# Other durations in the planner that orders a two-layer transformer on one core, and one buffer moved from weight sums to raw weights

## The chip, the cores and the metric

The kernel runs on one core of one Trainium2 chip. The metric is the device time of one execution in microseconds (us). The core has five engines that run side by side, each with an in-order queue of its own: PE (matmuls; the profile lists its weight loads apart, as PEld), DVE (element-wise work), ACT (element-wise functions, casts, copies out of PSUM), POOL and SP. Here SP issues every transfer between the chip's memory and the on-chip SBUF. Matmul results land in PSUM, eight banks of 128x512 numbers, and are read out by DVE or ACT. Engines wait for each other through semaphores.

## The reference

Two layers on 1024 tokens of width 1024, all in float32. Layer 0 mixes with sliding-window attention, layer 1 with a chunked linear recurrence (HGRN2); each is followed by a squared-ReLU MLP of width 4096.

```python
for layer in range(DEPTH):                       # DEPTH = 2
    h = rmsnorm(x, mix_norm[layer])
    if layer % 2 == 0:
        y = sliding_window_attention(h, positions, attn_w_qkv[0], attn_b_qkv[0], attn_sinks[0], attn_w_o[0])
    else:
        y = hgrn2_recurrence(h, lbs[layer], hgrn_w_in[0], hgrn_g_norm[0], hgrn_w_o[0])
    x = x + y
    h = rmsnorm(x, mlp_norm[layer])
    x = x + jnp.square(jax.nn.relu(h @ mlp_w_up[layer])) @ mlp_w_down[layer]
return rmsnorm(x, final_norm)
```

## The kernel before

**Arithmetic.** Activations lie as tiles of 128 features by 512 tokens (two halves of the sequence). A float32 product is made of three matmuls in the faster float32r format: each operand is split into a high part and the rest (`wh`, `wl` for a weight, two `a` or `t` tiles for an activation), and `mm3` adds high x high, high x rest and rest x high into one PSUM bank. `weight_split` makes `wh` by a cast (on ACT or on DVE, whichever the planner picks) and `wl` by a subtraction on DVE. The MLPs and the recurrence's input projection use Strassen's scheme (seven products for eight), in the up projections once more on some leaves; so weights are first added to each other (`strassen_weights`: sums s1 to s4 and the inner ones), and products are added up again by DVE.

**Stages in order of time.** Attention's projections and blocks (`qkv`, `attend`, `o_proj`), the first MLP (`pair_first`, `pair`, then `down`), the recurrence (`gates` and `recurrence`, one head after the other, interleaved), its output projection (`hgrn_out`), the second MLP, the final norm. Neighbouring stages overlap where their data allow.

**Buffers.** `BUFS` gives the number of SBUF tiles of each kind: 60 `a`, 18 `t`, 7 `m` (weight sums; also the softmax's scores and other short-lived tiles), 5 `wr` (raw weights as they come from memory), 5 `wh`, 5 `wl`; and 4 + 4 PSUM banks (`p`, `q`).

**What sets the order.** Nothing is issued while the code above runs: every operation is recorded with its engine (or two possible engines), a duration and what it reads and writes. `Schedule.order` then plays a list schedule: again and again it takes the engine that is free first, and of the operations that are ready there by its clock the one of lowest rank (program order; weights come 100 places earlier). A transfer occupies SP for its cost, and its data count as there `tail` later:

```python
            if op.form and op.form != form:
                form, t = op.form, t + DRAIN[op.form]
            free_at[e] = t + cost
            end = t + cost + op.tail
...
            for o in op.after:
                met(o, end + max(LATENCY[e][w] for w in o.ways))
...
                    heapq.heappush(slots[key], (b.freed + 200.0, b.slot))
```

The last line gives a buffer back when its last user has ended by that clock: a tile that is being stored keeps its slot until the planned landing of the store, and the next tile of that kind takes the slot that came free first. So the durations decide three things: the order in each engine's queue, the engine of each cast, and which slot a new tile gets, thus whose end it waits for on the chip. `DRAIN` is added in the plan where PE changes between matmuls that fill all 128 columns ("whole") and those that use half of them ("columns": attention's values and the recurrence's chunks). The order is then fixed in the program; on the chip each queue runs in that order, whatever the real durations are.

Of the kernel before, what the change touches and what calls it, by code (L numbers as in the profile page):

```python
# [37 lines left out]
MAGIC = 12582912.0  # L38
TWO_PI = (6.28125, 2029.0 / 2**20, 2 * np.pi - 6.28125 - 2029.0 / 2**20)
PI_DOWN = float(np.float32(3.1415925))  # L40
BUFS = {"a": 60, "t": 18, "m": 7, "sm": 8, "wr": 5, "wh": 5, "wl": 5, "p": 4, "q": 4}
CH = 64
LEVELS = 6
HOMES = "aaaaaaaaaaaa"
# [87 lines left out]
    "Pool": {"SP": 200.0, "PE": 190.0, "ACT": 75.0, "DVE": 74.0, "Pool": 102.0},  # L132
}
WEIGH = 1.0
DRAIN = {"whole": 120.0, "columns": 120.0}
LEAD = 100
WARM = 8
EVACUATE = 100
# [3 lines left out]
class Schedule:  # L142
# [42 lines left out]
    def order(self):  # L185
# [35 lines left out]
        while True:  # L221
# [36 lines left out]
# [3 lines that stand above are left out]
# [21 lines left out]
class Net:  # L282
# [38 lines left out]
    def a(self, dt=F32, shape=(P, TH)):  # L321
        return self.tile("a", BUFS["a"], shape, dt)

    def t(self, dt=F32, shape=(P, TH), tag="t"):
        return self.tile(tag, BUFS[tag], shape, dt)

    def psum(self, tag="p"):
        return self.tile(tag, BUFS[tag], (P, TH), F32, self.pp)

# [14 lines left out]
        return d  # L344

    def dma(self, out, in_, nbytes):
        self.op("SP", self.nc.sync.dma_start, [out], [in_], max(650.0, nbytes / 320.0), out, in_, tail=2000.0)

    def memset(self, out, value, e="DVE", late=()):
        self.op(e, self.engine(e).memset, [out], list(late), 300, out, value)  # L350
# [37 lines left out]

    def mm(self, out, lhsT, rhs, start, stop, n=TH, rate=1.0, form="whole", late=(), **kw):

        cost = n * rate / (2.25 if rate == 1.0 else 2.4) + 4
        self.op("PE", self.nc.tensor.matmul, [out], [lhsT, rhs, *late], cost, out, lhsT, rhs, start=start, stop=stop, form=form, **kw)

    def mm3(self, out, w, x, start, stop, n=TH, **kw):
# [12 lines left out]
    def raw(self, src):  # L407
        r = self.tile("wr", BUFS["wr"], (P, TH), F32)
        self.dma(r, src, 4 * P * TH)
        return r  # L410

    def weight_split(self, z):
        hi, lo = (self.tile(tag, BUFS[tag], (P, TH), F32R) for tag in ("wh", "wl"))
        self.copy(hi, z, TH, ("ACT", "DVE"), False)
        self.tt("any", lo, z, hi.bitcast(F32), ALU.subtract)
        return hi, lo
# [56 lines left out]
    def lay_out(self):  # L473
# [3 lines left out]
        for tag in ("a", "t", "wr", "wh", "wl"):  # L477
            for k in range(BUFS[tag]):
                self.pool.tile([P, TH], F32, tag=f"{tag}_{k}", name=f"{tag}_first{k}", bufs=1)
# [1175 lines left out]
```

## Time and profile before

| | |
|---|---|
| time, median of 3 runs | 2098.83 us (2096.93 to 2103.28) |
| the profiled execution's own time, and its span from first to last instruction | 2103.77 us, 2102.0 us |
| PE busy | 2068.4 us, 98% of the span, 12220 matmuls |
| DVE busy | 1898.4 us, 90% |
| ACT busy | 1120.0 us, 53% |
| transfers | 407.43 MB, 194 GB/s over the span |

The stages in the span, by the tiles that the trace shows: attention to about 350 us, first MLP to about 950 us, recurrence to about 1400 us, its output projection to about 1500 us, second MLP and final norm to 2102 us. All instructions carry the line of one helper (L336), so the profile is read by tile names and by time. A row of a view by time gives start, duration, engine, instruction, out<-in and, in square brackets, how long the engine stood idle before it and what ended that.

### The profile page before, as it was taken

The page shows a single profiled execution, that of the slowest core. Times are in us where ns is not written, and L with a number is a line of the kernel's source. Part 1 is how long each engine was busy: PE and PEld are TensorE (multiplying, and loading weights), DVE is VectorE, ACT ScalarE, POOL GpSimd, SP SyncE. Part 2 cuts the span into 40 slices and gives each one's busy share as a digit, 9 for nine tenths or more (in the row PEclk, how much of TensorE's full clock was granted, in tenths as well). Part 3 has the DMA queues.
Part 4 walks back from the last instruction along what each step waited for, and adds up shares of the span by engine and source line. Part 5 has one row for each costly group of instructions (what it writes and reads, how often), then busy time and mean ns, then how long its engine had stood idle before and what let it go on. Part 6 is the DMA issues. An engine that isn't in the chain of part 4 may idle for free.

```text
span 2102.0 us, 35648 instructions
## 1 busy us (share of the span) xinstructions
PE 2068.4 (98%) x12220; PEld 1738.6 (83%) x12220; DVE 1898.4 (90%) x3922; ACT 1120.0 (53%) x2284; POOL 61.0 (3%) x121
## 2 busy tenths in 40 slices
PE   9999999999999999999999999999999999999998
PEld 7778777888888887888888888888788888888887
DVE  8889899999999989999889888888999999998995
ACT  5567777656565323556444444443755656432453
POOL 4030000000000000000000000000000000000000
PEclk9999999999999999999999999999999999999999
DMA  6212277867778967732322232576787777896742
GB/s 214 79 51 81 86 239 245 297 224 248 231 240 289 313 220 245 236 136 76 101 98 99 96 101 97 202 234 221 270 267 229 244 228 250 284 321 211 238 133 80
DMA packets 225845, 407.43 MB, mean 194 GB/s; under 512 B 25344, under 2 KB 30464, under 8 KB 225664
## 3 DMA queue, kind: packets, MB, share of 16 engines
q1 hardware_dynamic: 225664, 405.16, 58.5%
q8 instruction: 96, 1.57, 0.3%
q14 instruction: 85, 0.70, 0.1%
HBM read 321.17 MB, written 83.89 MB: 193 GB/s over the span
## 4 chain that ended last, share of the span: by engine, by line
PE 38%; DVE 11%; DMA 4%; issue 3%; ACT 1%; POOL 0%; SPq 0%; POOLq 0%; DVEq 0%; ACTq 0%
PE p L336 22%; PE q L336 16%; DVE t L336 4%; DVE a L336 3%; DMA wr<-in_down 2%; DVE wl L336 2%; DVE m L336 2%; ACT t L336 1%; DMA t<-d 1%; DMA wr<-in_up 1%; DMA d<-t 0%; DVE wh L336 0%; DMA wr<-in_win 0%; DMA a<-d 0%; ACT wh L336 0%
## 5 line engine op out<-in xcount | busy, mean ns | idle before, releaser
L336 PE MATMUL p<-a,wh 128*128 128x512 f32 (+1 forms) x2880 | 809.9, 365 | 3.2 <-DVE a L336 2.4
L336 PE MATMUL q<-a,wh 128*128 128x512 f32 x2112 | 654.6, 391 | 7.4 <-ACT t L336 6.1
L336 PEld LDWEIGHTS p<-a,wh 128*128 128x128 f32 x2880 | 514.6, 189 | 89.1 <-DVE a L336 4.0
L336 PE MATMUL p<-a,wl 128*128 128x512 f32 (+1 forms) x1440 | 521.0, 362 | 0.4 <-DVE wl L336 0.4
L336 PEld LDWEIGHTS q<-a,wh 128*128 128x128 f32 x2112 | 389.1, 188 | 85.3 <-ACT t L336 8.4
L336 PE MATMUL q<-a,wl 128*128 128x512 f32 x1056 | 411.1, 390 | 1.7 <-DVE wl L336 1.7
L336 PEld LDWEIGHTS p<-a,wl 128*128 128x128 f32 x1440 | 271.6, 189 | 40.9 <-DVE wl L336 1.3
L336 DVE TENSOR_TENSOR wl<-wr,wh 128x512 fp32r<-128x512 f32 x352 | 240.8, 685 | 6.7 <-ACT wh L336 1.3
L336 DVE TENSOR_TENSOR wl<-m,wh 128x512 fp32r<-128x512 f32 x338 | 230.1, 686 | 10.6 <-ACT wh L336 1.4
L336 PEld LDWEIGHTS q<-a,wl 128*128 128x128 f32 x1056 | 198.3, 188 | 45.6 <-DVE wl L336 3.7
L336 ACT ACTIVATE t<-t 128x512 f32<-128x512 f32 x268 | 168.8, 632 | 122.3 <-DVE t L336 114.9
L336 ACT CAST wh<-wr 128x512 fp32r<-128x512 f32 x249 | 154.0, 619 | 142.8 <-PE p L336 94.7
L336 DVE TENSOR_TENSOR t<-t,t 128x512 f32<-128x512 f32 (+3 forms) x337 | 197.4, 599 | 17.0 <-DMA t<-d 9.9
L336 ACT CAST a<-t 128x512 fp32r<-128x512 f32 (+1 forms) x216 | 130.1, 611 | 148.5 <-PE q L336 78.7
L336 DVE TENSOR_TENSOR a<-t,a 128x512 fp32r<-128x512 f32 (+2 forms) x314 | 205.9, 677 | 2.2 <-ACT a L336 1.7
L336 ACT CAST wh<-m 128x512 fp32r<-128x512 f32 x231 | 143.1, 620 | 113.8 <-PE p L336 47.4
L336 ACT COPY t<-q 128x512 f32<-128x512 f32 (+2 forms) x201 | 112.2, 559 | 104.1 <-PE q L336 87.3
L336 DVE TENSOR_TENSOR m<-wr,wr 128x512 f32<-128x512 f32 (+1 forms) x188 | 120.9, 645 | 17.6 <-DMA wr<-in_down 13.0
L336 PE MATMUL p<-wh,a 128*128 128x512 f32 x384 | 124.9, 396 | 0.7 <-ACT a L336 0.7
L336 DVE TENSOR_TENSOR t<-t,p 128x256 f32<-128x256 f32 x294 | 118.0, 414 | 0.3
L336 PEld LDWEIGHTS q<-t,t 128*64 128x64 f32 (+1 forms) x2160 | 95.4, 144 | 13.6 <-issue 7.6
L336 PE MATMUL q<-t,t 128*64 128x32 f32 (+2 forms) x2160 | 105.3, 229 | 0.0
(129 smaller groups left out, 2392.7 us busy)
## 6 DMA issues: line engine op xcount, KB each, us to landing
t<-d SPq DMA_DIRECT2D x548, 256.0 KB, 4.1
d<-t SPq DMA_DIRECT2D x244, 256.0 KB, 2.7
wr<-in_down SPq DMA_DIRECT2D x224, 256.0 KB, 4.2
wr<-in_up SPq DMA_DIRECT2D x178, 256.0 KB, 3.9
wr<-in_win SPq DMA_DIRECT2D x68, 256.0 KB, 2.9
a<-d SPq DMA_DIRECT2D x60, 256.0 KB, 4.7
wr<-in_wqkv SPq DMA_DIRECT2D x48, 256.0 KB, 2.9
d<-a SPq DMA_DIRECT2D x48, 256.0 KB, 3.9
```

Of the source, the lines that this page charges most:

```text
L336: fn(*[place(a) for a in args], **{k: place(v) for k, v in kw.items()})
```

## The change

Numbers of the plan change, and two of the buffer counts; no operation is added or taken away.

```diff
-BUFS = {"a": 60, "t": 18, "m": 7, "sm": 8, "wr": 5, "wh": 5, "wl": 5, "p": 4, "q": 4}
+BUFS = {"a": 60, "t": 18, "m": 6, "sm": 8, "wr": 6, "wh": 5, "wl": 5, "p": 4, "q": 4}
...
-DRAIN = {"whole": 120.0, "columns": 120.0}
+DRAIN = {"whole": 200.0, "columns": 200.0}
+FULL = {512: 227.3, 256: 119.8}
...
     def dma(self, out, in_, nbytes):
-        self.op("SP", ..., max(650.0, nbytes / 320.0), out, in_, tail=2000.0)
+        self.op("SP", ..., max(450.0, nbytes / 320.0), out, in_, tail=2750.0)
...
     def mm(self, out, lhsT, rhs, start, stop, n=TH, rate=1.0, form="whole", late=(), **kw):
-        cost = n * rate / (2.25 if rate == 1.0 else 2.4) + 4
+        cost = FULL.get(n, n / 2.25 + 4) if rate == 1.0 else n * rate / 2.4 + 4
```

In the plan, a float32r matmul over 512 columns now lasts 227.3 ns where it lasted 231.6, over 256 columns 119.8 where it was 117.8; a transfer's data come 2750 ns after its issue's end where it was 2000; an issue lasts at least 450 ns where it was 650 (a transfer of 256 KB stays at 262144 / 320 = 819 ns, so only small ones change); a change of form costs 200 ns where it was 120. A sixth raw weight tile is loaded ahead in `first_loads`, and one weight sum fewer can be alive.

What this does to the queues, at two places. The digits before the underscore number a tile; they are the same in both kernels there.

The start of the second MLP, ACT's queue, before. `q4300` is a PSUM bank with a finished product; the copy into `t4302` empties it so that PE can go on.

```order
L336 ACTIVATE t4230_17987<-q4092_17552 128x512
L336 COPY a4240_17996<-t4236_17886 128x512
L336 COPY wh4322_18002<-wr4315_17897 128x512
L336 COPY t4260_18018<-t4248_17903 128x512
L336 COPY t4268_18026<-t4249_17993 128x512
L336 COPY wh4324_18032<-m4311_17946 128x512
L336 COPY t4303_18043<-q4301_17998 128x512
L336 COPY t4302_18057<-q4300_17930 128x512
L336 COPY t4264_18065<-t4248_17903 128x512
```

The same place after the change:

```order
L337 ACTIVATE t4230_17982<-q4092_17541 128x512
L337 COPY a4240_17991<-t4236_17886 128x512
L337 COPY wh4322_17997<-wr4315_17892 128x512
L337 COPY t4260_18014<-t4248_17932 128x512
L337 COPY t4302_18022<-q4300_17927 128x512
L337 COPY wh4324_18028<-m4311_17963 128x512
L337 COPY t4268_18039<-t4249_18011 128x512
L337 COPY t4264_18056<-t4248_17932 128x512
L337 COPY t4304_18071<-q4300_17927 128x512
L337 COPY t4303_18083<-q4301_17993 128x512
```

The copy out of `q4300` moved three rows forward. The slot of `t4302` changed too: before, it was that of `t4230`, and the copy had to wait until the store of `t4230` to memory had landed; now it is a slot whose last user is a DVE operation.

PE's queue at the same place, before (the matmuls from `wh4296` on write `q4300` again, so they wait for that copy):

```order
L336 MATMUL q4340_18034<-a3939_16732,wh4320_17981 128x512
L336 MATMUL q4340_18034<-a3940_16766,wh4320_17981 128x512
L336 MATMUL p4343_18041<-a3955_16857,wh4322_18002 128x256
L336 MATMUL p4343_18041<-a3956_16867,wh4322_18002 128x256
L336 MATMUL p4344_18046<-a3963_16968,wh4322_18002 128x256
L336 MATMUL p4344_18046<-a3964_16978,wh4322_18002 128x256
L336 MATMUL q4341_18052<-a4098_17188,wh4324_18032 128x512
L336 MATMUL q4341_18052<-a4099_17203,wh4324_18032 128x512
L336 MATMUL q4300_17930<-a4128_17330,wh4296_17906 128x512
L336 MATMUL q4300_17930<-a4129_17340,wh4296_17906 128x512
```

And after:

```order
L337 MATMUL q4340_18030<-a3939_16744,wh4320_17973 128x512
L337 MATMUL q4340_18030<-a3940_16766,wh4320_17973 128x512
L337 MATMUL q4300_17927<-a4128_17351,wh4296_17899 128x512
L337 MATMUL q4300_17927<-a4129_17376,wh4296_17899 128x512
L337 MATMUL q4300_17927<-a4128_17351,wl4297_17911 128x512
L337 MATMUL q4300_17927<-a4130_17399,wh4296_17899 128x512
L337 MATMUL q4300_17927<-a4131_17439,wh4296_17899 128x512
L337 MATMUL q4300_17927<-a4130_17399,wl4297_17911 128x512
```

The six matmuls into `p4343`, `p4344` and `q4341` moved behind the twelve that write `q4300`.

The end of the recurrence's output projection, DVE's queue, before. `m4211` is a weight sum of the second MLP, for which ACT and PE wait; the `a` tiles are splits of activations, `t4160` a sum of squares.

```order
L336 TENSOR_TENSOR t4156_17494<-t4156_17494,t4109_17313 128x512
L336 TENSOR_TENSOR t4160_17522<-t4160_17522,t4161_17529 128x512
L336 TENSOR_TENSOR m4210_17699<-wr4208_17514,wr4209_17536 128x512
L336 TENSOR_TENSOR a4154_17706<-t4152_17474,a4153_17691 128x512
L336 TENSOR_TENSOR t4160_17522<-t4160_17522,t4162_17550 128x512
L336 TENSOR_TENSOR a4158_17718<-t4156_17494,a4157_17708 128x512
L336 TENSOR_TENSOR t4160_17522<-t4160_17522,t4163_17600 128x512
L336 TENSOR_TENSOR m4211_17730<-m4210_17699,wr4206_17485 128x512
```

And after:

```order
L337 TENSOR_TENSOR t4156_17528<-t4156_17528,t4109_17308 128x512
L337 TENSOR_TENSOR a4137_17673<-t4096_17111,a4136_17657 128x512
L337 TENSOR_TENSOR a4150_17678<-t4148_17487,a4149_17664 128x512
L337 TENSOR_TENSOR wl4197_17684<-wr4183_17406,wh4196_17676 128x512
L337 TENSOR_TENSOR t4160_17586<-t4160_17586,t4161_17623 128x512
L337 TENSOR_TENSOR a4154_17696<-t4152_17507,a4153_17686 128x512
L337 TENSOR_TENSOR a4158_17703<-t4156_17528,a4157_17693 128x512
L337 TENSOR_TENSOR t4160_17586<-t4160_17586,t4162_17594 128x512
L337 TENSOR_TENSOR m4210_17715<-wr4208_17479,wr4209_17494 128x512
L337 TENSOR_TENSOR t4160_17586<-t4160_17586,t4163_17628 128x512
L337 TENSOR_TENSOR m4211_17730<-m4210_17715,wr4206_17427 128x512
```

`a4137`, which stood 26 rows ahead of `m4211`, is now 9 rows ahead of it. Counted from `wl4193`, the subtraction that stands some twenty rows earlier in both kernels, `m4211` is the 22nd row before and the 24th after.

Elsewhere the PE queue is nearly unchanged outside attention. In DVE's queue up to the norm ahead of the first MLP, 36 casts from `wr` to `wh` stand where 23 stood; over the whole program DVE has 263 casts where it had 273. SP issues the same 1560 transfers; loads of weights and stores of activations change places by some rows.

More of the change, by code (lines that the diff above doesn't have):

```diff
@@ L346, in dma @@
     def dma(self, out, in_, nbytes):
-        self.op("SP", self.nc.sync.dma_start, [out], [in_], max(650.0, nbytes / 320.0), out, in_, tail=2000.0)
+        self.op("SP", self.nc.sync.dma_start, [out], [in_], max(450.0, nbytes / 320.0), out, in_, tail=2750.0)
     def memset(self, out, value, e="DVE", late=()):
```

## The prediction

> **What bounds the kernel now.** I read the page's busy times first, then PE's waits, then the windows of the stages, then the places of the longest waits in the view by time.
>
> ```profile
> PE 2068.4 (98%) x12220; PEld 1738.6 (83%) x12220; DVE 1898.4 (90%) x3922; ACT 1120.0 (53%) x2284; POOL 61.0 (3%) x121
> PE q L336 <- ACT t L336: 8.9, 11, 2.5
> PE q L336 <- DVE t L336: 3.5, 5, 1.0
> PE q L336 <- DVE a L336: 2.7, 5, 1.6
> PE p L336 <- DVE a L336: 2.4, 2, 1.5
> PE q L336 <- DVE sm L336: 1.7, 2, 1.4
> PE q L336 <- DVE wl L336: 1.7, 3, 0.9
> PE q L336 <- DVE m L336: 1.5, 4, 0.6
> PE p L336 <- DVE t L336: 1.5, 2, 1.2
> PE q L336 <- ACT wh L336: 1.2, 1, 1.2
> PE p L336 <- ACT a L336: 0.7, 1, 0.7
> PE p L336 <- ACT t L336: 0.5, 1, 0.5
> PE p L336 <- DVE wl L336: 0.4, 1, 0.4
> ```
>
> A row of waits reads: who, for whom, us in total, times, longest. PE stands idle 2102.0 - 2068.4 = 33.6 us, and the twelve rows add up to 26.7 of them; the rest lies at the start and the end. No row names a transfer: PE waits for DVE and ACT alone, in some forty places. The change leaves the number of matmuls as it is, so a gain can only come out of these 26.7 us, and a loss has no such bound.
>
> ```profile
> core 0: us, PE busy (x) PEld busy (x) DVE busy (x) ACT busy (x) POOL busy (x), PEclk, DMA share, GB/s
> 50.00:350.00 300.00, 292.45 (x1605) 232.18 (x1604) 268.27 (x579) 204.15 (x578) 22.72 (x49) 1.00 0.39 125
> 500.00:600.00 100.00, 100.00 (x606) 89.57 (x605) 92.40 (x196) 59.39 (x100) 0.00 (x0) 1.00 0.73 238
> 950.00:1400.00 450.00, 445.79 (x3798) 370.59 (x3798) 396.90 (x903) 214.85 (x467) 8.90 (x18) 1.00 0.35 118
> 1998.61 43.52 PE q L336 x192
> ```
>
> In the up projections (500 to 600 us) PE never stops. Attention (50 to 350 us) and the seam between the recurrence and the second MLP are where it waits. The last row, of the chain, is a stretch of matmuls with nothing between them: 43.52 / 192 = 226.7 ns each. The old plan took 231.6, the new one takes 227.3. So the old plan's PE ran 2% late against the chip's, and its DVE order was made for a PE that asks later.
>
> **Place 1, start of the second MLP (gain).**
>
> ```profile
> 1515.95 5.41 DMA d<-t
> 1517.94 0.62 ACT L336 CAST wh<-m 128x512 fp32r<-128x512 f32 x1
> 1518.38 0.64 PE L336 MATMUL p<-a,wh 128*128 128x256 f32 x4
> 1520.80 0.41 DVE L336 TENSOR_TENSOR m<-wr 128x256 f32<-128x256 f32 x1
> 1521.38 0.58 ACT L336 COPY t<-q 128x512 f32<-128x512 f32 x1 [2.35 <-DMA d<-t]
> 1522.02 0.73 PE L336 MATMUL q<-a,wh 128*128 128x512 f32 x2 [2.54 <-ACT t L336]
> 1522.52 0.69 DVE L336 TENSOR_TENSOR t<-t,t 128x512 fp32r<-128x512 f32 x1 [1.31 <-ACT t L336]
> 1525.21 0.50 PE L336 MATMUL q<-a,wl 128*128 128x512 f32 x1 [0.17 <-DVE wl L336]
> t<-d SPq DMA_DIRECT2D x548, 256.0 KB, 4.1
> d<-t SPq DMA_DIRECT2D x244, 256.0 KB, 2.7
> ```
>
> The copy that empties `q4300` takes the slot of a tile whose store is on its way; the store takes 5.41 us, ACT stands for 2.35, and PE for 2.54. With the new slot and the new row, the copy follows `t4260` directly, in the place where ACT now does its next cast, and ends by about 1518.1, ahead of PE's 1518.38. Then twelve matmuls run (12 x 0.227 = 2.7 us, to 1521.1) while ACT copies `q4300` out again, and the six displaced ones (2 x 0.227 + 4 x 0.16 = 1.1 us) cover that copy's 0.58. What is late next is `wl4321`: DVE no longer stands 1.31 us behind ACT, so from 1521.2 on it has four rows of 0.34 to 0.6 and the subtraction itself, done by 1523.5, and PE asks at 1524.9. In exchange `t4303` now waits for a store, of `t4260`; behind it in ACT's queue stand two casts and a copy whose results PE needs only after these 24 matmuls. Price: -2.54 - 0.17 = **-2.7 us**; no better than that, and 0 if a store is slow at the new place.
>
> The Trainium skill, DMA: Bandwidth & Descriptors (Anatomy of one DMA), gives a transfer a fixed 2.0 us or so and its bytes at 436 GB/s, which as an estimate is 2.6 us for 256 KB; by it the old plan's 0.82 + 2.0 was right already and the new 0.82 + 2.75 holds slots too long. The rows above speak against it for loads (4.1 us) and this store, and for it at the median store (2.7 us).
>
> **Place 2, end of the recurrence's output projection (loss).**
>
> ```profile
> 1492.39 0.69 DVE L336 TENSOR_TENSOR m<-m,wr 128x512 f32<-128x512 f32 x1
> 1492.99 0.68 DVE L336 TENSOR_TENSOR t<-t,t 128x512 f32<-128x512 f32 x1
> 1493.78 0.73 PE L336 MATMUL q<-a,wh 128*128 128x512 f32 x2 [1.22 <-ACT wh L336]
> 1495.53 0.73 PE L336 MATMUL q<-a,wh 128*128 128x512 f32 x2 [1.01 <-ACT t L336]
> ```
>
> DVE issues one such row every 0.60 us (1492.99 - 1492.39). `m4211` stands two rows later than before, counted from `wl4193`, so the cast and both of PE's waits behind it end 2 x 0.60 = **+1.2 us** later. If DVE comes to `wl4193` earlier than before, the price is 0; if it comes with a further row of arrears, 1.8.
>
> **Place 3, start of the first MLP (nothing, net).**
>
> ```profile
> 337.57 0.68 DVE L336 TENSOR_TENSOR t<-p,t 128x512 f32<-128x512 f32 x1
> 341.25 0.74 PE L336 MATMUL q<-a,wh 128*128 128x512 f32 x2 [2.09 <-ACT t L336]
> 347.33 0.83 PE L336 MATMUL q<-c,t 128*128 128x1 f32 x6 [0.99 <-DVE t L336]
> ```
>
> The first wait is for a copy that stands on ACT behind a cast, itself behind a DVE subtraction; five of DVE's rows go behind that subtraction, the two ACT steps on the tile of 337.57 stay ahead of the copy, and it ends 1.0 us earlier. The second wait is for the last addition of a sum of squares: in the new DVE queue it is the eighteenth row after that of 337.57, so it ends near 337.57 + 0.68 + 18 x 0.60 = 349.1; PE has eight more matmuls ahead of it (1.8 us) and comes 1.0 earlier, at 346.3 - 1.0 + 1.8 = 347.1, and waits 2.0 where it waited 0.99. **0 us**, between -1.0 and +1.0.
>
> **Down projections and recurrence.**
>
> ```profile
> 815.71 0.50 PE L336 MATMUL p<-a,wh 128*128 128x512 f32 x1 [1.50 <-DVE a L336]
> 1965.90 0.50 PE L336 MATMUL p<-a,wh 128*128 128x512 f32 x1 [0.88 <-DVE a L336]
> 952.10 0.73 PE L336 MATMUL p<-a,wh 128*128 128x512 f32 x2 [0.53 <-ACT t L336]
> ```
>
> The splits behind the first two rows stand some rows nearer to the pass's start; an earlier split of the same pass stands later. I take -0.6 of the 1.50 and nothing of the 0.88; ends -2.4 and +1.0. At 952 the copy has, net, 1.8 us more of ACT's rows ahead of it, on an ACT that is busy for 215 of 450 us in this stretch: +1.0, between 0 and 1.8. In five of the eight heads of the recurrence, two matmuls (0.45 us) more stand between a transposition and the matmul that waits for its copy: I take -1.0, a quarter of the 4.2 us that PE stands idle there (450 - 445.8); ends 0 and -2.3 (5 x 0.45). Two waits for `wl` in the down projections shrink by half a row each, -0.5; ends 0 and the 1.7 of their row.
>
> **Attention.**
>
> ```profile
> L336 DVE CAST wh<-wr 128x512 fp32r<-128x512 f32 x103 | 43.5, 422 | 26.0 <-PE p L336 20.4 <-DMA wr<-in_wqkv 2.9 <-PE q L336 2.4
> ```
>
> Thirteen casts more on DVE are 13 x 0.42 = 5.5 us, beside 300 - 268.3 = 31.7 us that DVE stands idle there. PE's queue changes too: between the score matmuls of a block and the transpositions of its probabilities stand, summed over the 32 blocks and priced at 0.227 and 0.12 us a matmul, 4.9 us of other matmuls more than before: 12.5 more in some blocks, 7.6 fewer in eleven. PE stands idle for 7.55 us in the stretch (300 - 292.45), 3.1 of them at place 3. I take -1.0, since cover of 0.15 us a block is nearer to nothing than to either end: bounds -4.5 (all idle time gone) and +5.5 (every added cast in PE's way; the second rival goes further).
>
> **What costs nothing.** In the up projections one slot for sums fewer makes DVE do a subtraction ahead of the next sum, by rows of 0.6; the cover is that weights wait for PE, not PE for weights (PE 100.00 of 100). If it were gone, DVE has 7.6 us in 100 to give. A sixth raw weight lands earlier, which no wait of PE asks for; SP issues the same transfers, at 35% to 73% of the DMA engines' time in the windows above, and a store that moves behind loads is read back in a later stage. The 200 ns for a change of form only move the plan's clock.
>
> **Sum.** -2.7 + 1.2 + 0 - 0.6 + 1.0 - 1.0 - 0.5 - 1.0 = **-3.6 us**. The profiled execution took 2103.8 us (span 2102.0), 4.9 over the median of the runs, 2098.8; I take the sum off the median: **2095.2 us**. A measurement of this kernel tells about 0.3%, 6.3 us, from no change; the sum is inside that; all ends at once would reach from -15 to +11.
>
> **Rivals.**
> *The plan now fits everywhere.* With PE's pace right to 0.3%, DVE's order suits the real PE not only at the places that I read but at most of the forty. Half of the 26.7 us would go: 2098.8 - 13.4 = 2085.4. For it: the 226.7 ns; against: place 2, and the 18 rows of place 3.
> *DVE holds PE up in attention.* The casts stand in the in-order queue ahead of a block's mask, maximum and normalisation, and eleven blocks lose 7.6 us of cover. If both land on PE: 7.6 + 5.5 = 13.1, less the 2.6 that the other places leave, 2098.8 + 10.5 = 2109.3. It decides for slower from 8.9 of these 13.1 us on. For it: DVE busy 89% there, PE's waits there are for DVE; against: 31.7 us idle DVE, and the longer cover elsewhere.
> *The gain at place 1 was one slow store.* In another execution that store may land in the median 2.7 us, and nothing is gained there: 2098.8 - 0.9 = 2097.9, no change. The rule of the Trainium skill above would say so.
>
> **How the numbers follow.** The sum's case has 0.50, of which 0.18 lies over 6.3 us faster and 0.32 within; the fitting plan 0.22, all faster; DVE in attention 0.25, all slower; the slow store 0.03, within. Faster 0.40, same 0.35, slower 0.25. The range holds the sum's case with most of its ends, the fitting plan's nearer half and beyond its middle, and DVE's case up to its full price: 2084 to 2109; the likeliest case's own range is 2088 to 2104.
>
> **What would show it.** Right: no PE wait for ACT over 1 us near 1520; PE's waits at the seam before the second MLP about 1 us longer; PE 100 of 100 in the up projections; PE busy 2068 and a span shorter by the waits alone. Wrong: PE's idle time in 50 to 350 us above 13, or waits for `wl` or `m` in the up projections, or a transfer among PE's releasers.

## The result and the profile after

The changed kernel takes 2086.74 us (median of 6 runs, 2085.56 to 2088.37); the kernel before, beside it, 2098.48 us (median of 6, 2096.90 to 2103.28). The ratio is 0.9943 (95% interval 0.9932 to 0.9954): 0.57% or 11.7 us faster. The forecast was 2095.2 with 2084 to 2109: the sign and the range held, and the gain is three times the sum of the terms, 3.6. It also lies outside the 2088 to 2104 that the prediction gave its likeliest case alone.

The page of the changed kernel, first its busy times, then the chain that ended last:

```profile
span 2084.9 us, 35687 instructions
PE 2062.8 (99%) x12220; PEld 1741.4 (84%) x12220; DVE 1893.6 (91%) x3919; ACT 1122.4 (54%) x2280; POOL 59.8 (3%) x121
PE 90%; DVE 5%; issue 2%; ACT 1%; DMA 1%; SPq 0%; POOLq 0%; POOL 0%; DVEq 0%; ACTq 0%
```

PE stands idle 2084.9 - 2062.8 = 22.1 us, where it was 33.6, and the chain runs through PE for 90% of the span. PE's waits in the changed kernel (us in total, times, longest):

```profile
PE q L337 <- ACT t L337: 3.4, 4, 1.3
PE q L337 <- DVE a L337: 2.6, 5, 1.6
PE q L337 <- DVE t L337: 2.6, 4, 0.9
PE p L337 <- DVE wl L337: 1.8, 3, 1.1
PE q L337 <- DVE sm L337: 1.7, 2, 1.4
PE p L337 <- DVE t L337: 1.2, 1, 1.2
PE q L337 <- DVE wl L337: 1.0, 1, 1.0
PE p L337 <- ACT t L337: 0.8, 2, 0.5
PE q L337 <- DVE m L337: 0.4, 1, 0.4
PE q L337 <- ACT m L337: 0.2, 1, 0.2
```

They sum to 15.7 us in 24 places, against 26.7 in 38. The larger change is one step back, in what DVE waits for. First the rows of the kernel before that name a transfer and have more than 1.5 us, then those of the changed kernel:

```profile
DVE m L336 <- DMA wr<-in_down: 13.0, 15, 1.7
DVE t L336 <- DMA t<-d: 9.9, 11, 2.3
DVE m L336 <- DMA wr<-in_up: 6.4, 9, 1.9
DVE a L336 <- DMA a<-d: 6.0, 2, 3.1
DVE a L336 <- DMA wr<-in_down: 3.4, 5, 0.8
DVE wh L336 <- DMA wr<-in_wqkv: 2.9, 1, 2.9
DVE m L336 <- DMA wr<-in_win: 1.9, 2, 1.5
```

```profile
DVE wh L337 <- PE q L337: 52.1, 84, 1.5
...
DVE wh L337 <- DMA wr<-in_wqkv: 2.6, 1, 2.6
DVE m L337 <- DMA wr<-in_down: 1.6, 4, 0.7
DVE a L337 <- DMA a<-d: 0.8, 2, 0.6
...
DVE m L337 <- DMA wr<-in_up: 0.3, 1, 0.3
```

All rows of DVE that name a transfer sum to 44.7 us before and 5.7 after. DVE is as busy as it was (1898.4 and 1893.6); it now waits for PE to give back a weight slot (52.1 us in the row with `q`, 19.6 before), that is, it is ahead. The transfers themselves are no faster. The page's issues after, in KB each and median us to landing:

```profile
t<-d SPq DMA_DIRECT2D x548, 256.0 KB, 4.3
d<-t SPq DMA_DIRECT2D x244, 256.0 KB, 2.8
wr<-in_down SPq DMA_DIRECT2D x224, 256.0 KB, 4.2
```

The two rows that the prediction showed of before were 4.1 and 2.7.

### The profile page after: what moved, and what is told of

It is laid out like the page before. It is cut to its first block, busy times and chain, and to the rows that moved or that the text cites. A ratio compares the mean times of both kernels' runs of the same rounds, so it can differ in the third digit from the quotient of the medians.

```text
span 2084.9 us, 35687 instructions
## 1 busy us (share of the span) xinstructions
PE 2062.8 (99%) x12220; PEld 1741.4 (84%) x12220; DVE 1893.6 (91%) x3919; ACT 1122.4 (54%) x2280; POOL 59.8 (3%) x121
## 4 chain that ended last, share of the span: by engine, by line
PE 90%; DVE 5%; issue 2%; ACT 1%; DMA 1%; SPq 0%; POOLq 0%; POOL 0%; DVEq 0%; ACTq 0%
PE p L337 47%; PE q L337 43%; DVE t L337 2%; DVE a L337 2%; DVE wl L337 1%; ACT a L337 1%; DMA a<-d 0%; DVE m L337 0%; DMA a<-in_x 0%; ACT t L337 0%; DMA wr<-in_up 0%; ACT wh L337 0%; SPq L337 0%; ACT m L337 0%; DMA wr<-in_wo 0%
## 5 line engine op out<-in xcount | busy, mean ns | idle before, releaser
L337 ACT ACTIVATE t<-t 128x512 f32<-128x512 f32 x254 | 159.8, 632 | 111.2 <-DVE t L337 105.2
L337 ACT CAST wh<-m 128x512 fp32r<-128x512 f32 x240 | 149.1, 622 | 124.1 <-PE q L337 60.4
L337 DVE TENSOR_TENSOR t<-t,p 128x256 f32<-128x256 f32 x294 | 117.8, 420 | 0.0
```

Source lines behind the costliest of these rows:

```text
L337: fn(*[place(a) for a in args], **{k: place(v) for k, v in kw.items()})
```

## The experiments

The theories were: **durations fit** (the plan's times, nearer to the chip's, take PE's waits away; by PE's pace or by the transfers' landing), **sixth raw weight** (the slot does it), and **scatter** (each order falls by chance, and the one before was unlucky). "Before" is measured beside each set: 2099.97 us for e1 to e4, 2103.83 for e5 to e8, 2103.34 for e9 to e12. Absolute times of two sets stand side by side only roughly; a ratio is always to "before" of the same set.

**e1: the new slots alone.** Edit against the changed kernel:

```diff
-DRAIN = {"whole": 200.0, "columns": 200.0}
+DRAIN = {"whole": 120.0, "columns": 120.0}
-        ... max(450.0, nbytes / 320.0), out, in_, tail=2750.0)
+        ... max(650.0, nbytes / 320.0), out, in_, tail=2000.0)
-        cost = FULL.get(n, n / 2.25 + 4) if rate == 1.0 else n * rate / 2.4 + 4
+        cost = n * rate / (2.25 if rate == 1.0 else 2.4) + 4
```

> The old durations with the new slots (m 6, wr 6); nothing is left out of the computation. Theory 'durations fit' (the plan's matmul, transfer and form-change times, nearer to the chip's, took PE's waits away): 2098, within 3 us of the kernel before, PE's named waits near 26. Theory 'sixth raw weight' (a load that may start one tile earlier took away DVE's 13.0 us of waits for wr, and with them PE's): near 2087, all of the gain, DVE's waits for wr under 3 us. Theory 'scatter' (any other order lands anywhere between about 2085 and 2105, with no part of the change to thank): a time that fits neither, for instance over 2102.

Measured: 2094.73 us (2090.93 to 2095.64), ratio 0.9967 (0.9954 to 0.9979). Neither number came: it is a little over half of the gain. DVE's waits for the down projection's weights fell from 13.0 to 5.7 us, and ACT took up waits of its own. Rows of e1, DVE's and ACT's waits:

```profile
DVE m L337 <- DMA wr<-in_down: 5.7, 6, 1.7
...
ACT t L337 <- DMA wr<-in_up: 16.4, 11, 2.2
```

ACT's row had 2.8 us before. The slot lets a load start earlier, but the plan still believes 2.0 us of landing.

**e2: the new durations alone.**

```diff
-BUFS = {... "m": 6, "sm": 8, "wr": 6, ...}
+BUFS = {... "m": 7, "sm": 8, "wr": 5, ...}
```

> The new durations with the old slots (m 7, wr 5); nothing is left out. 'Durations fit': 2087 to 2090, DVE's waits for wr back at up to 13 us without PE waiting more. 'Sixth raw weight': near 2098, DVE's waits for wr near 13 us and PE's named waits near 26. 'Scatter': no relation to e1; the gains of e1 and e2 do not add up to 11.7 us by more than 4.

Measured: 2088.92 us (2088.64 to 2091.24), ratio 0.9944 (0.9930 to 0.9957). All of the gain within the intervals, and inside the 2087 to 2090 of "durations fit"; on top of the new durations the slots bring nothing that these runs resolve. The gains of e1 (0.33%) and e2 (0.56%) overlap, so they are largely the same waits.

**e3: all but the matmul times.**

```diff
-        cost = FULL.get(n, n / 2.25 + 4) if rate == 1.0 else n * rate / 2.4 + 4
+        cost = n * rate / (2.25 if rate == 1.0 else 2.4) + 4
```

> All of the change but the matmul times: 231.6 and 117.8 ns in the plan again, where the chain of before shows 226.7 for 512 columns; nothing is left out. 'Durations fit', by way of PE's pace: 2093 to 2098, PE's waits in many small places back. By way of the transfers: 2087 to 2089. 'Sixth raw weight': 2087 to 2089. 'Scatter': anywhere, with the long waits at other places than in either kernel.

Measured: 2090.98 us (2090.34 to 2091.51), ratio 0.9952 (0.9939 to 0.9964), 2 us over the band of "by way of the transfers" and 2 below that of "PE's pace". The interval overlaps the full change's.

**e4: all but the transfer times.**

```diff
-        ... max(450.0, nbytes / 320.0), out, in_, tail=2750.0)
+        ... max(650.0, nbytes / 320.0), out, in_, tail=2000.0)
```

> All of the change but the transfer times: at least 650 ns of issue and 2000 ns of landing again, so 2.8 us for 256 KB where the chip's medians are 2.7 to 4.3; nothing is left out. 'Durations fit', by way of the transfers: 2093 to 2098, and DVE and ACT stand for transfers again (before: 13.0 us for wr, 6.4 for m from in_up, 9.9 for t). By way of PE's pace: 2087 to 2089 with those waits of DVE back and off PE's path. 'Sixth raw weight': 2087 to 2089. 'Scatter': anywhere.

Measured: 2092.07 us (2091.03 to 2093.22), ratio 0.9958 (0.9945 to 0.9970), 1 us short of the band. e3 and e4 cannot be told apart: leaving out one part leaves most of the gain. ACT's wait for `wr<-in_up` was 19.5 us here, so the transfers' part was felt, but a study by leaving out did not settle it. Single parts and doses had to.

**e5 and e6: the kernel before, 50 ns to either side.**

```diff
-        ... max(650.0, nbytes / 320.0), out, in_, tail=2000.0)
+        ... max(650.0, nbytes / 320.0), out, in_, tail=1950.0)     (e6: tail=2050.0)
```

> The kernel before with one number of its plan moved by 50 ns: a transfer's landing takes 1950 instead of 2000 ns, further from the chip's 2.7 to 4.3 us; slots and all else as before; nothing is left out. 'Durations fit': 2098 to 2101, within 3 us of the kernel before, since 50 ns is nothing against what it is wrong by. 'Scatter' (each order lands by chance between about 2085 and 2105, and the order before was an unlucky one): several us from the kernel before, likelier down than up, 2090 to 2097.

> The same the other way: 2050 instead of 2000 ns of landing in the kernel before, a step toward the chip's; nothing is left out. 'Durations fit': 2097 to 2100, within 3 us of the kernel before. 'Scatter': several us from it and from e5, 2090 to 2097.

Measured: e5 2107.50 us (2104.09 to 2109.48, 12 runs), ratio 1.0018 (1.0008 to 1.0029); e6 2100.85 us (2095.02 to 2104.96, 12 runs), ratio 0.9985 (0.9973 to 0.9998). The shorter landing is 3.7 us worse and the longer one 3.0 better: more than "durations fit" allowed, and not what "scatter" said, since neither median came near 2090 to 2097.

**e7 and e8: the changed kernel, 50 ns to either side.**

```diff
-        ... max(450.0, nbytes / 320.0), out, in_, tail=2750.0)
+        ... max(450.0, nbytes / 320.0), out, in_, tail=2700.0)     (e8: tail=2800.0)
```

> The changed kernel with a landing of 2700 instead of 2750 ns; nothing is left out. 'Durations fit': within 2 us of the changed kernel, 2086 to 2090, and of e8. 'Scatter': 2090 to 2097, since the changed kernel's order would then be a lucky one; PE's named waits back at 20 or more.

> The same the other way: 2800 instead of 2750 ns in the changed kernel; nothing is left out. 'Durations fit': 2086 to 2090, within 2 us of e7. 'Scatter': over 3 us from e7 or from the changed kernel.

Measured: e7 2087.06 us (2085.79 to 2087.52), ratio 0.9924 (0.9908 to 0.9939); e8 2086.33 us (2085.41 to 2086.78), ratio 0.9921 (0.9904 to 0.9938). Both stand within 0.5 us of the changed kernel's 2086.74 (another set), although their orders differ from its. The two neighbours of the old plan lie 6.7 us apart, those of the new one 0.7. The 6.7 are more than a slope can explain, since the whole step of 750 ns brought about 10 (e10): some chance of the order is in them. But three orders near the old plan are all slow and three near the new one all fast, so the gain is no lucky order; "scatter" as its cause fell here.

**e9: the kernel before with the new matmul times alone.**

```diff
-        cost = n * rate / (2.25 if rate == 1.0 else 2.4) + 4
+        cost = FULL.get(n, n / 2.25 + 4) if rate == 1.0 else n * rate / 2.4 + 4
```

> The kernel before with the new matmul times alone (227.3 and 119.8 ns; old transfer times, form changes and slots); nothing is left out. 'PE's pace was the fault': 2088 to 2092 where before gives 2098 to 2104, and the runs lie as close together as those of the changed kernel (within 3 us). 'Landing was the fault' (the plan let DVE and ACT ask for a transfer 0.7 to 2 us before it lands): 2097 to 2104, DVE's waits for wr, m and t from transfers as before (near 30 us), runs still spread over 5 us or more.

Measured: 2102.72 us (2098.89 to 2106.62, 12 runs), ratio 0.9996 (0.9983 to 1.0008): nothing. A row of e9's DVE waits, then PE by time in the first down projection:

```profile
DVE m L337 <- DMA wr<-in_down: 14.4, 12, 2.0
```

```profile
817.26 0.80 PE L337 MATMUL p<-a,wh 128*128 128x512 f32 x1 [4.40 <-DVE a L337]
```

With PE's pace right and the landing wrong, DVE stands for transfers as before (45.9 us over all rows), and PE's wait for an activation's split at the start of this pass, 1.50 us before, is 4.40. (The profiled execution of e9 was the slowest of its twelve.)

**e10: the kernel before with the new transfer times alone.**

```diff
-        ... max(650.0, nbytes / 320.0), out, in_, tail=2000.0)
+        ... max(450.0, nbytes / 320.0), out, in_, tail=2750.0)
```

> The kernel before with the new transfer times alone (2750 ns of landing, 450 of issue at least; old matmul times and slots); nothing is left out. 'Landing was the fault': 2088 to 2092, runs within 3 us of each other, DVE's waits for transfers under 12 us. 'PE's pace was the fault': 2097 to 2104 and runs spread as before. Both contribute: 2091 to 2096 here and in e9.

Measured: 2093.17 us (2091.82 to 2095.39), ratio 0.9949 (0.9931 to 0.9967). By the ratio this is nine tenths of the gain; by the absolute time, 1 us over the band of "landing" and inside that of "both" (which e9 missed). The runs spread over 3.6 us, not 3, and DVE's waits for transfers are 17.7 us over all rows, not under 12 as "landing" said; with the sixth slot and the form change added (e3) they are 10.3. In e10 as in e4 the least time of an issue goes with the landing. It touches only the 27 of 1560 transfers that are of 128 KB or less, and was not tried apart.

**e11 and e12: the changed kernel with a landing of 1200 and of 3400 ns.**

```diff
-        ... max(450.0, nbytes / 320.0), out, in_, tail=2750.0)
+        ... max(450.0, nbytes / 320.0), out, in_, tail=1200.0)     (e12: tail=3400.0)
```

> The changed kernel with a landing of 1200 instead of 2750 ns, further off than the old 2000; nothing is left out. 'Landing was the fault': worse than e4's 0.9958 of the kernel before, 2094 to 2102, and runs spread over 4 us or more. 'PE's pace was the fault': 2087 to 2091.

> The changed kernel with a landing of 3400 ns, so 4.2 us for 256 KB, the median that the trace shows for loads; nothing is left out. 'Landing was the fault': 2084 to 2087, with DVE's and ACT's waits for transfers smaller still; the gain is small since PE's waits for transfers' followers are nearly gone. A loss, 2089 to 2095, would say that slots held longer in the plan cost more than the safer landing brings.

Measured: e11 2103.61 us (2101.06 to 2107.99, 12 runs), ratio 1.0004 (0.9992 to 1.0016): with PE's pace, the form change and the slots all new, the whole gain is gone, and the time is 1.6 us above the band of "landing". e12 2084.96 us (2083.89 to 2085.94), ratio 0.9910 (0.9890 to 0.9929), the lowest of all and inside its band; it was not run beside the changed kernel, and 1.8 us between two sets settles nothing but that it is no worse. How a landing that the plan takes too short reaches PE, in e11 by time in the second down projection:

```profile
1763.66 3.55 SPq L337 DMA_DIRECT2D wr<-in_down  x2
1766.16 0.69 DVE L337 TENSOR_TENSOR m<-wr,wr 128x512 f32<-128x512 f32 x1 [2.92 <-DMA wr<-in_down]
...
1767.97 0.41 DVE L337 TENSOR_TENSOR t<-t,p 128x256 f32<-128x256 f32 x1
1768.53 0.48 PE L337 MATMUL p<-a,wh 128*128 128x256 f32 x2 [2.50 <-DVE t L337]
```

DVE stands 2.92 us before a weight sum. Behind that sum in its queue is the row that reads a bank `p`, and PE waits 2.50 us for it. PE's row names `DVE t`, not the transfer.

The runs in one table. The waits are sums over all rows of a view that name a transfer, in the profiled execution. The last two columns come from the same traces, whose rows were put beside the numbered tiles of each kernel's program: for the 739 to 752 loads that DVE is the first to use, the lead is the time from the issue to the moment at which DVE has come to that row. "Short leads" is the value under which one lead in twenty lies, and "too early" counts the loads that DVE came to before they had landed.

| kernel | planned landing, matmul, wr | us | max - min of runs (n) | DVE for transfers | PE idle | short leads, us | too early |
|---|---|---|---|---|---|---|---|
| e11 | 1200, new, 6 | 2103.6 | 6.9 (12) | 38.6 | 33.0 | 3.35 | 42 |
| e5 | 1950, old, 5 | 2107.5 | 5.4 (12) | 42.7 | 32.0 | 3.58 | 56 |
| before | 2000, old, 5 | 2098.5 to 2103.8 (four sets) | 11.0 (23, beside e5) | 44.7 | 33.6 | 3.58 | 48 |
| e9 | 2000, new, 5 | 2102.7 | 7.7 (12) | 45.9 | 33.2 | 3.58 | 50 |
| e6 | 2050, old, 5 | 2100.9 | 9.9 (12) | 38.5 | 25.5 | 3.58 | 46 |
| e1 | 2000, old, 6 | 2094.7 | 4.7 (5) | 26.0 | 26.1 | 3.62 | 27 |
| e4 | 2000, new, 6 | 2092.1 | 2.2 (5) | 21.3 | 25.2 | 4.10 | 25 |
| e10 | 2750, old, 5 | 2093.2 | 3.6 (6) | 17.7 | 26.8 | 3.96 | 27 |
| e2 | 2750, new, 5 | 2088.9 | 2.6 (5) | 14.6 | 24.6 | 4.00 | 23 |
| e3 | 2750, old, 6 | 2091.0 | 1.2 (5) | 10.3 | 23.1 | 4.70 | 11 |
| e7 | 2700, new, 6 | 2087.1 | 1.7 (6) | 7.3 | 20.9 | 4.70 | 9 |
| changed | 2750, new, 6 | 2086.7 | 2.8 (6) | 5.7 | 22.1 | 4.70 | 8 |
| e8 | 2800, new, 6 | 2086.3 | 1.4 (6) | 10.4 | 23.1 | 4.75 | 14 |
| e12 | 3400, new, 6 | 2085.0 | 2.1 (5) | 4.3 | 21.7 | 5.31 | 4 |

With slots and matmul times new, the time falls with the planned landing from 1200 to 2700 ns (2103.6, 2092.1, 2087.1); from there to 3400 (2086.7, 2086.3, 2085.0) these runs resolve no step. What the landing and the sixth slot have in common is the lead: both make loads start longer before DVE asks for them, at different ends. The slot lifts the middle (the median lead is 9.7 to 10.4 us in the six kernels with five slots and 11.1 to 12.2 in the eight with six); the planned landing lifts the shortest leads, and those make DVE wait, since a load takes about 4 us. That is the cause that the runs show; PE's pace is not one by itself. ACT's waits for transfers (50.3 us before, 32.0 after, but 64.1 in e1 and 61.5 in e4) do not follow the time. Nor do DVE's in every execution: that of e6, among its quickest at 2095.22 us, has 38.5 us of them and only 25.5 of idle PE. Whether the matmul times and the form change bring a little on top of the landing (e10 against e2: 4 us in different sets, but 0.9949 against 0.9944 by the ratios) stays open, and the form change was not tried alone.

## Why the prediction was right in sign and too small

The bound was read rightly in the main: the gain came for the most part out of PE's waits for DVE and ACT, which fell by 26.7 - 15.7 = 11.0 us, and no operation went. First rows of the kernel before by time: DVE where it stands for a transfer, a wait of PE behind the first of them, and ACT at place 2. Then the places in the changed kernel, rows of DVE, PE and ACT picked out by time; then its stages of attention and recurrence, with the columns of the prediction's windows (the recurrence's work lies about 6 us earlier there):

```profile
725.60 0.69 DVE L336 TENSOR_TENSOR m<-wr,wr 128x512 f32<-128x512 f32 x1 [1.64 <-DMA wr<-in_down]
727.95 0.50 PE L336 MATMUL q<-a,wl 128*128 128x512 f32 x1 [0.67 <-DVE wl L336]
...
797.00 0.69 DVE L336 TENSOR_TENSOR a<-m,a 128x512 f32<-128x512 f32 x1 [3.14 <-DMA a<-d]
...
1493.11 0.62 ACT L336 CAST wh<-m 128x512 fp32r<-128x512 f32 x1 [2.39 <-DVE m L336]
```

```profile
333.55 0.70 DVE L337 TENSOR_TENSOR t<-p,t 128x512 f32<-128x512 f32 x1
344.37 0.70 DVE L337 TENSOR_TENSOR t<-t,t 128x512 f32<-128x512 f32 x1
344.53 0.50 PE L337 MATMUL q<-a,wl 128*128 128x512 f32 x1 [1.00 <-DVE wl L337]
...
1478.39 0.73 PE L337 MATMUL q<-a,wh 128*128 128x512 f32 x2 [1.10 <-ACT t L337]
1482.92 0.62 ACT L337 CAST wh<-m 128x512 fp32r<-128x512 f32 x1 [0.58 <-DVE m L337]
1485.34 0.73 PE L337 MATMUL q<-a,wh 128*128 128x512 f32 x2 [0.76 <-ACT t L337]
...
1507.14 0.58 ACT L337 COPY t<-q 128x512 f32<-128x512 f32 x1
1507.73 1.07 PE L337 MATMUL q<-a,wh 128*128 128x512 f32 x4
1511.91 0.59 ACT L337 COPY t<-q 128x512 f32<-128x512 f32 x1 [0.22 <-DMA d<-t]
```

```profile
50.00:350.00 300.00, 294.78 (x1616) 235.91 (x1615) 274.40 (x598) 199.23 (x568) 24.05 (x52) 0.99 0.38 130
944.00:1394.00 450.00, 447.44 (x3816) 374.07 (x3815) 398.69 (x904) 218.47 (x477) 8.24 (x18) 1.00 0.34 119
```

- **Place 1**, -2.7: right in mechanism and size. The copy out of `q4300`, at 1507.14, stands for nothing, and PE's matmuls behind it (1507.73) do not stop: 2.54 and 0.17 are gone, -2.7. The copy at 1511.91 is `t4303`, which now waits for a store, as said: 0.22 us, and not in PE's way. (The four narrow matmuls that I priced at 0.16 us took 0.12 each, 1518.38 to 1518.85 in the trace of before; nothing hung on it.)
- **Place 2**, +1.2: failed. The wait of 1.22 us for the cast of `m4211` is gone: that cast stood 2.39 us for its sum before and 0.58 after (1482.92), though the sum stands two rows later. DVE comes there earlier by more than two rows, the case for which I had named a price of 0. The wait of 1.01 for a copy became 0.76, and a wait of 1.10 for another copy, at 1478.39, is new: -0.4 in all.
- **Place 3**, 0: failed. 2.09 + 0.99 became the one wait of 1.00 at 344.53, for another tile: -2.1. The eighteen rows were counted rightly, but the row from which I counted starts at 333.55 and not at 337.57. So the addition that I put at 349.1 starts at 344.37, is done at 345.07, and holds PE up no more.
- **Down projections**, -0.6: mis-sized. The waits of 1.50 and 0.88 are gone: -2.4. So are the two for `wl`, -0.5 in the sum: 0.67 at 727.95 and 0.88 at 1878.82, together -1.55.
- **952 us**, +1.0: 0.53 became 0.46, so -0.1. **Heads**, -1.0: right. The waits of 0.20 to 0.22 us for a transposition's copy in five heads (at 1090, 1145, 1199, 1254 and 1309 us before) are gone, -1.1. With the stretch's other waits, PE's idle time in the recurrence went from 4.2 to 450 - 447.44 = 2.56, -1.6 without the row at 952.
- **Attention**, -1.0: idle 7.55 - 3.08 (place 3) = 4.47 before, 300 - 294.78 - 1.00 = 4.22 after, -0.25. The thirteen casts on DVE cost nothing: the second rival, 2109.3, did not happen.

The terms make -11.1 of the 11.5 us by which PE's idle time fell; the rest is two waits that no term named (0.28 at 386 us and 0.46 at 1561 us), both gone, less 0.3 more in the first 50 us. The profiled spans differ by more, 17.1, because the profiled execution of before lay 5.3 us above its median and because PE's busy time fell too, from 2068.4 to 2062.8. Part of that can be estimated: a matmul's record lasts 0.40 us at a pitch of 0.227, so each stop hides 0.17 us under the record ahead of it; fourteen stops fewer are 2.4 us. The other 3.2 are many small delays: by the starts of the matmuls in the two traces, delays of under 0.18 us each, which show as no idle time, came to 3.8 us less; what they are I have not traced. "PE busy 2068 and a span shorter by the waits alone" was wrong.

**The step that failed** is one: "no row names a transfer", and from it "a sixth raw weight lands earlier, which no wait of PE asks for". I read who released PE and stopped there. One step further back DVE stood 44.7 us for transfers, in an in-order queue with 7.6 us in 100 to spare in the up projections. At places 2 and 3 and in the down projections DVE had stood for a transfer ahead of PE's wait, and from there on it had not stood idle again: 1.94 us at 326 ahead of place 3, 2.28 and 1.78 at 1444 and 1455 ahead of place 2, 1.64 at 725.60 and 1.37 at 1877 right ahead of the two waits for `wl`, 3.14 at 797.00 and 2.87 at 1947 (each with another 0.7 us eight us later) ahead of the two for splits. Of all these, 0.29, 0.20 and 0.65 us are left after the change, ahead of place 3 and of the two splits. I put the new order's rows on the old trace's clock, at 0.60 us a row, and so kept those arrears: places 2, 3 and the down projections all came out too late. (At place 3 the transfer explains 1.65 of the 4.0 us by which DVE is earlier; the rest came with the new order and an earlier PE, and was not taken apart.) Place 1, the one place where I followed the wait back to a transfer, came out right.

**The rival that the plan fits everywhere** gave 2085.4, 1.3 us from the result, and its half of the waits is near what happened (11.0 of 26.7). Its reason was wrong: it rested on PE's pace, and e9 shows that worth nothing alone. So the nearness of its number is luck. **The slow store** as the only gain (2097.9) fell with the time itself; the store's wait at place 1 stayed away, and so did others that it doesn't touch.

The weighing of the transfers' rule can now be closed by the series above: each step of the planned landing up to 3400 ns, which makes 0.82 + 3.4 = 4.2 us, the median of the `in_down` loads, made the time shorter or left it. The Trainium skill, DMA: Bandwidth & Descriptors (Anatomy of one DMA), whose fixed 2.0 us and 436 GB/s give an estimate of 2.6 us for 256 KB, would have called the old 2.82 us right; it fits these figures on transfers issued from GpSimd, and all here are issued from SP. The measurement decides against it for the loads of `t` (4.1 us before), `in_down` (4.2) and `in_up` (3.9), while those of `in_win` and `in_wqkv` (2.9) and the stores (2.7) lie near it.

## What to carry to other kernels

Read waits two steps back: when PE waits for DVE, ask what DVE stood for, because an in-order queue that has stood for a transfer, with little idle time to catch up in, is late at the rows behind it, and PE's small waits there carry another name. In a static order, plan a transfer with the landing that the loaded chip shows in the trace, not the best one; planning up to the loads' median of 4.2 us cost nothing here, and 1200 ns instead (e11 against e12, one set) cost 19 us. Before reading a gain out of a list schedule, run the neighbours of both plans: here they were the cheapest proof against luck.

## What the runs showed of the hardware that was not expected

The landing of a 256 KB load hardly changed with the order in the three traces read for it: `t<-d` took a median 4.1 us before, 4.3 after, 4.4 in e12. And kernels whose DVE stands for transfers for 38 us or more spread over 5.4 to 13 us from run to run (before, e5, e6, e9, e11), while all those at 26 us or less stay within 4.7 over 5 or 6 runs each; before spread 6.4 over 6 runs. That landings which vary between executions make this spread fits, but was not measured.
